# A decoder block on one core: the memory's keys and values kept on chip, the first output weights split first, the tokens' low parts made by VectorE, and the first gather written by token tiles

## The chip, the core and the metric

The kernel runs on one core of one Trainium2 chip. A core has four compute engines that each work through their own list in order: TensorE (PE in the profile, with PEld for its weight loads), VectorE (DVE), ScalarE (ACT) and GpSimd (POOL). SyncE (SP) only issues transfers, and GpSimd issues some as well; each engine's transfers start in the order of its list. The metric is the time of one execution in microseconds on the device; lower is better.

## The reference, cut to what matters

One decoder layer on 512 tokens of width 1024, in float32. The mixing stage projects the normed tokens, runs two branches (an RWKV-7 recurrence and a sparse attention), lifts and gates both and projects their sum. Then come cross-attention to 256 memory tokens and a mixture of 32 experts, of which each token uses 2.

```python
def hybrid_layer(h, mem, ...):
    z = rmsnorm(h, norm_mix) @ w_in
    z_rw, z_dsa, z_gate = _split(z, (RW_COLS, DSA_COLS, GATE_COLS))
    y_a = rwkv7_branch(z_rw, ...)
    y_b = dsa_branch(z_dsa, kv_norm, w_uk, w_uv)
    g_a, g_b = jnp.split(jax.nn.sigmoid(z_gate + b_gate), 2, axis=-1)
    h = h + (g_a * (y_a @ w_proj_a) + g_b * (y_b @ w_proj_b)) @ w_out
    h = h + cross_attention(rmsnorm(h, norm_cross), rmsnorm(mem, norm_mem), w_cq, w_ckv, w_co)
    h = h + hier_moe(rmsnorm(h, norm_ffn), ...)
    return h

def cross_attention(hn, mem_n, w_cq, w_ckv, w_co):
    q = (hn @ w_cq).reshape(B, S, X_HEADS, X_HEAD_DIM)
    k, v = jnp.split((mem_n @ w_ckv).reshape(B, M, 2, X_HEADS, X_HEAD_DIM), 2, axis=2)
    ...
    s = jnp.einsum('bshd,bmhd->bhsm', q, k).astype(jnp.float32) * (X_HEAD_DIM ** -0.5)
    p = jax.nn.softmax(s, axis=-1).astype(v.dtype)
    o = jnp.einsum('bhsm,bmhd->bshd', p, v).reshape(B, S, X_WIDTH)
    return o @ w_co

def hier_moe(hn, w_rg, b_rg, w_re, b_re, w_gate, w_up, w_down):
    g_prob = jax.nn.softmax((xt @ w_rg + b_rg).astype(jnp.float32), axis=-1)
    p_grp, grp = lax.top_k(g_prob, 1)
    ...
    p_e, e_loc = lax.top_k(jax.nn.softmax(e_logits, axis=-1), TOP_K_INNER)
    gate = p_grp * p_e / jnp.sum(p_e, -1, keepdims=True)
    ...
        hid = jax.nn.silu(xb @ w_gate[e]) * (xb @ w_up[e])
        return (hid @ w_down[e]) * gts[:, None].astype(xb.dtype)
```

## The kernel before, in words

All of it is one program for one core. Operands of a matmul are split into a high part (a rounded copy, `float32r`) and a low part (the rest), and a product is three matmuls: high by high, high by low, low by high. `split` makes both parts: ScalarE casts the high one, VectorE (or GpSimd, where the call says G) subtracts for the low one. Tokens are four tiles of 128 (`NT` = 4), features eight blocks of 128 (`KD` = 8).

The stages, with their place in the span of the profile: norms and transposes (0 to 40 us), the input projection with the recurrence and the indexer (40 to 390), the sparse attention `attend` (390 to 485), with the projection of the memory's keys as filler between its matmuls, the projection of the memory's values (485 to 513), the two lifts `w_pa` and `w_pb` (520 to 566), `w_out` (566 to 614), the queries, weights and values of the cross-attention (614 to 691), `w_co` with the routing (691 to 751), the first gather (751 to 765), the experts (766 to 1230) and the last norm.

Order. The program is written in the order of the stages, and a list scheduler then orders each engine's instructions; inside `tc.manual_schedule(engines={PE.engine})` TensorE keeps the written order. `behind(x)` makes what follows wait in the scheduler's list for instruction x. `M` is a free-list allocator over one big tile: `get` takes a place (with `top=True` from the upper end) and `done` gives it back; an instruction that writes to a place used before waits for that place's last readers and writers. `psum` takes the eight banks of PSUM in turn, by groups.

Memory's keys and values. `keys_values` loads 256 KB pieces of `w_ck` and `w_cv` through `ringm` (four raw buffers, two pairs of parts), which SyncE issues. ScalarE copies each result out of PSUM into a staging tile, and GpSimd's queue stores it to `kT_d` and `vm_d` in DRAM. After the lifts SyncE loads both back into `kT` and `vm`, and four splits of `kT` (cast by ScalarE, subtraction by GpSimd) make `kP`, the keys in two parts.

The lifts. For each of `w_pa` and `w_pb` the four blocks of the branch's output (`yaT`, `ybT`) are split into `act`, then four weights of 512 KB come through `ring2` (four raw buffers, three pairs of parts), each used for two groups of twelve matmuls. GpSimd's queue loads the gates from `gate_d`, and VectorE multiplies by them out of PSUM.

The routing. `tokmajor(w_co, ...)` writes a token tile at a time; after each, `after_cross` computes the logits (TensorE transposes L1079, logits L1083), adds them up (L1139, L1140), and `route` (L1089 to L1098) picks the group and the two experts on VectorE in steps of 4 to 32 columns. `parts` writes the token tile in two parts: ScalarE the high part (L1122) and a second full copy (L1123), GpSimd the difference (L1124). `place` (matmuls L1104, L1105) counts the tokens of earlier tiles for each expert, so that a token gets its row in the expert's block; tile t's placement needs tile t's choice.

The first gather. `choose(0)` makes a matrix of zeros and ones for the first four experts (L1166, one instruction for each token tile), and `gather(0, k)` multiplies the tokens by it: for each feature block k, a bank, eight matmuls over four token tiles and two parts, then a scaling by VectorE or ScalarE into `xgs`. All 64 matmuls carry line L1421. Then `turned` transposes the split gates (L1210) and the experts begin (L1452).

## Time and profile before

| | us |
|---|---|
| median of the timed runs (3) | 1271.01 |
| lowest and highest | 1266.04, 1273.87 |
| the profiled execution | 1261.12 |
| its span, first to last instruction | 1259.3 |
| TensorE busy | 1186.5 |
| VectorE, ScalarE, GpSimd busy | 647.8, 366.6, 111.1 |
| mean granted clock of TensorE | 0.965 of full speed |

The profiled execution is one run, 0.8% below the median of the timed ones; times inside the program are read from it. TensorE is busy 94% of the span, so an engine's work matters where TensorE waits for it. A granted clock of 1.00 is 2.4 GHz, one of 0.50 is 1.2 GHz.

### The profile page before, as it was taken

What the parts mean: (1) busy time and instruction counts of PE and PEld (TensorE: products, weight loads), DVE (VectorE), ACT (ScalarE), POOL (GpSimd) and SP (SyncE); (2) the same over time, 40 slices, a digit from 0 to 9 for tenths busy, and PEclk for the clock granted to TensorE, in tenths of its full rate; (3) what the DMA queues carried; (4) which work ended last, traced back from release to release, by engine and by line L of the source; (5) the groups of instructions that cost most, each with busy time, mean ns of one, the idle gap of its engine ahead of it and who ended that gap; (6) DMA issues with size and microseconds to landing.
All of it is one profiled execution on the core that took longest, in us unless ns stands there. A gap on an engine that the chain in (4) does not pass through costs nothing. (4 is left out here: it accounts for less than half of the span.)

```text
span 1259.3 us, 18869 instructions
## 1 busy us (share of the span) xinstructions
PE 1186.5 (94%) x7630; PEld 860.6 (68%) x7630; DVE 647.8 (51%) x1417; ACT 366.6 (29%) x666; POOL 111.1 (9%) x102
## 2 busy tenths in 40 slices
PE   5999998899998999799999979899999999999995
PEld 5877676677777877688786867566565656565662
DVE  5346689686686563565545373433233333333325
ACT  4442322434333543422444351101010101110113
POOL 1121211111122101200000030000000000000001
PEclk8999898999998999899999989999999999999998
DMA  4211113215533115473324316899999999999991
GB/s 163 91 60 34 54 56 109 79 53 185 193 113 109 55 34 196 155 245 98 131 75 145 128 68 268 337 413 419 419 421 420 420 421 421 419 421 420 362 364 67
DMA packets 52137, 272.06 MB, mean 216 GB/s; under 512 B 6064, under 2 KB 6208, under 8 KB 27728
## 3 DMA queue, kind: packets, MB, share of 16 engines
q1 hardware_dynamic: 48544, 259.21, 53.5%
q0 software_dynamic: 3504, 11.62, 2.6%
q8 instruction: 61, 1.00, 0.3%
q14 instruction: 28, 0.23, 0.1%
HBM read 261.37 MB, written 9.44 MB: 215 GB/s over the span
## 5 line engine op out<-in xcount | busy, mean ns | idle before, releaser
L230 PE MATMUL banks<-xparts 128*128 128x512 f32 x864 | 227.0, 413 | 2.2 <-DVE xparts L197 2.2
L230 PEld LDWEIGHTS banks<-xparts 128*128 128x128 f32 x864 | 164.5, 196 | 43.2 <-issue 3.7
L1452 PE MATMUL banks<-big 128*64 128x256 f32 x1616 | 180.3, 380 | 0.0
L1452 PEld LDWEIGHTS banks<-big 128*64 128x64 f32 x1616 | 115.8, 137 | 63.5 <-issue 8.0
L230 PE MATMUL banks<-weights,rounded 128*128 128x512 f32 x384 | 95.0, 401 | 0.0
L1480 PE MATMUL banks<-big 128*64 128x512 f32 x384 | 86.6, 595 | 1.4 <-issue 1.4
L230 PEld LDWEIGHTS banks<-weights,rounded 128*128 128x128 f32 x384 | 72.0, 191 | 15.2 <-issue 1.0
L1364 DVE TENSOR_TENSOR big<-big,banks 128x512 f32<-128x512 f32 x128 | 79.6, 681 | 4.7 <-PE banks L1362 4.7
L1457 ACT ACTIVATE slot<-banks 128x256 f32<-128x256 f32 x32 | 12.3, 385 | 225.0 <-PE banks L1469 121.1
L197 ACT CAST xparts<-rawring 128x1024 fp32r<-128x1024 f32 x38 | 39.8, 1046 | 121.0 <-PE banks L230 61.3
L1421 PE MATMUL banks<-chosen,rounded 128*128 128x256 f32 x512 | 66.0, 290 | 0.5 <-DVE big L1139 0.3
L197 DVE TENSOR_TENSOR weights<-big,weights 128x1024 fp32r<-128x1024 f32 x32 | 39.0, 1222 | 53.6 <-ACT weights L197 51.2
L1362 PE MATMUL banks<-chosen 128*128 128x512 f32 x256 | 66.5, 403 | 0.0
L1356 DVE SCALAR_TENSOR_TENSOR chosen<-banks,big,chosen 128x512 fp32r<-128x512 f32 x32 | 24.0, 750 | 82.2 <-ACT chosen L1355 82.2
L1421 PEld LDWEIGHTS banks<-chosen,rounded 128*128 128x128 f32 x512 | 64.5, 198 | 2.2 <-DVE big L1438 1.2
L1480 PEld LDWEIGHTS banks<-big 128*64 128x64 f32 x384 | 26.9, 137 | 53.1 <-issue 48.4
L197 POOL TENSOR_TENSOR xparts<-rawring,xparts 128x1024 fp32r<-128x1024 f32 x20 | 48.9, 2446 | 150.4 <-ACT xparts L197 142.7
L1355 ACT ACTIVATE chosen<-banks,big 128x512 fp32r<-128x512 f32 x32 | 22.0, 688 | 131.3 <-PE banks L1480 121.0
L1470 DVE COPY big<-banks 128x512 f32<-128x512 f32 x16 | 11.1, 692 | 89.5 <-PE banks L1469 89.5
L197 ACT CAST weights<-big 128x1024 fp32r<-128x1024 f32 x32 | 33.4, 1051 | 79.6 <-PE banks L230 33.4
L1362 PEld LDWEIGHTS banks<-chosen 128*128 128x128 f32 x256 | 47.7, 192 | 11.9 <-issue 1.6
L1437 DVE TENSOR_SCALAR chosen<-banks,big 128x512 fp32r<-128x512 f32 x16 | 12.0, 751 | 81.9 <-PE banks L1435 81.9
(406 smaller groups left out, 1808.7 us busy)
## 6 DMA issues: line engine op xcount, KB each, us to landing
big<-in_w_e_gate SPq DMA_DIRECT2D x51, 1024.0 KB, 13.5
big<-in_w_e_up SPq DMA_DIRECT2D x50, 1024.0 KB, 13.6
big<-in_w_e_down SPq DMA_DIRECT2D x48, 1024.0 KB, 12.4
rawring<-in_w_in SPq DMA_DIRECT2D x38, 512.0 KB, 3.5
slots<-in_w_e_up SPq DMA_DIRECT2D x14, 1024.0 KB, 15.2
slots<-in_w_e_gate SPq DMA_DIRECT2D x13, 1024.0 KB, 13.4
slots<-in_w_e_down SPq DMA_DIRECT2D x12, 1024.0 KB, 11.7
big<-in_x SPq DMA_DIRECT2D x8, 512.0 KB, 6.4
```

The source lines that it names most:

```text
L197: return S.copy(hi, src).ins, (eng or V).tensor_tensor(lo, src, hi.bitcast(F32), op=OP.subtract).ins
L230: r = PE.matmul(pt, st(a), mv(b), start=(first and i == 0), stop=(last and i == 2))
L1355: r = S.activation(YE[:, 0, nh, :], pd, AF.Copy, scale=g[:, :])
L1356: V.scalar_tensor_tensor(YE[:, 1, nh, :], pd, g[:, :], YE[:, 0, nh, :].bitcast(F32), op0=OP.mult, op1=OP.subtract)
L1362: PE.matmul(pc_[:, :], PT[:, t * P:(t + 1) * P], YE[:, x, nh, :], start=(x == 0), stop=(x == 1))
L1364: V.tensor_add(hh, hh, pc_[:, :])
L1421: PE.matmul(pt[:, 0:256], HL(x, t)[:, k // 4, k % 4, :], Pr_[:, t].rearrange("p e s -> p (e s)"), start=(t == 0 and x == 0), stop=(t == NT ...
L1437: V.tensor_scalar(PT[:, :], pa[:, :], slot_id[:, :], None, op0=OP.is_equal)
L1452: PE.matmul(pu[x][hf * 64:hf * 64 + 64, :], xgs[h4][:, k % 4, es_], w[:, k % 4, hf * 256:hf * 256 + 256], start=(k == 0), stop=(k == KD - 1))
L1457: S.activation(hd_[:, :], pu[0], AF.Silu)
L1470: V.tensor_copy(ht[:], ph[:, :].rearrange("p (j a s) -> p j a s", j=2, s=64))
L1480: PE.matmul(pd[j * 64:j * 64 + 64, :], ht[:, j, fb * 2 + hf, :], w[hf][j][:, fb, nh * 512:nh * 512 + 512], start=(kb == 0), stop=(kb == 3))
```

## The change

It has four parts.

1. `kT` and `vm` get their places in `M` before the attention, once the recurrence's tiles are given back, and ScalarE copies the results out of PSUM straight into them. The DRAM tiles, the twelve stores and the two loads are gone.
2. The first weight of `w_pa` is loaded and split ahead of the four blocks of `yaT`; the three products of each lift come in the order high by high, low weight by high tokens, high weight by low tokens. The splits of `kT` are put behind the last matmul of the first group of `w_pa`.
3. In `parts` the low part is one VectorE instruction (scale, then subtract the high part); ScalarE's second copy and GpSimd's subtraction are gone.
4. The first gather keeps four PSUM banks for all eight feature blocks and goes by token tiles: choice of tile t, then its 16 matmuls, with the placement of the last tile ahead of the last 16. `first_gather` then does the eight scalings.

```diff
+    for x in (St[0], St[1], Sp, *Xs, AR, ZV, ST, AA, zxg, g2, msk, pc):
+        x.done()
+    kT, vm = M.get(KD, NMEM, top=True), M.get(2, D, top=True)
...
-            S.copy(kst[nb % 2][:, :], pt[:, 0:NMEM])
-            nc.gpsimd.dma_start(kT_d[:, nb, :], kst[nb % 2][:, :])
+            S.copy(kT[:, nb, :], pt[:, 0:NMEM])
...
-                S.copy(vst[t][:, :], pts[t][:, :])
-                nc.gpsimd.dma_start(vm_d[:, t, half * 512:half * 512 + 512], vst[t][:, :])
+                S.copy(vm[:, t, half * 512:half * 512 + 512], pts[t][:, :])
...
+        w0 = ring2.load(wsrc[0]) if x == 0 else None
         for k in range(4):
             split(act[:, x, 0, k, :], act[:, x, 1, k, :], src[:, k, :])
         for j in range(4):
-            w = ring2.load(wsrc[j])
+            w = w0 if x == j == 0 else ring2.load(wsrc[j])
...
-                for a, b in ((0, 0), (0, 1), (1, 0)):
+                for a, b in ((0, 0), (1, 0), (0, 1)):
...
+                if x == nb == 0:
+                    first_pa = r.ins
...
-    kT, vm = M.get(KD, NMEM, top=True), M.get(2, D, top=True)
-    nc.sync.dma_start(kT[:, :, :], kT_d[:, :, :])
-    nc.sync.dma_start(vm[:, :, :], vm_d[:, :, :])
-    for k in range(0, KD, 2):
-        split(kP[:, 0, k:k + 2, :], kP[:, 1, k:k + 2, :], kT[:, k:k + 2, :], G)
+    with behind(first_pa):
+        for k in range(0, KD, 2):
+            split(kP[:, 0, k:k + 2, :], kP[:, 1, k:k + 2, :], kT[:, k:k + 2, :], G)
...
-            S.activation(hn[:, g], src, AF.Copy, scale=rs[:, t:t + 1])
-            G.tensor_tensor(lo, hn[:, g], hi.bitcast(F32), op=OP.subtract)
+            V.scalar_tensor_tensor(lo, src, rs[:, t:t + 1], hi.bitcast(F32), op0=OP.mult, op1=OP.subtract)
...
-    place(NT - 1)
...
-    chosen = choose(0)
+    gathered = [PS[:, i, :] for i in (2, 3, 4, 5)]
+    first = {}
+    with tc.manual_schedule(engines={PE.engine}):
+        for t in range(NT):
+            if t == NT - 1:
+                place(t)
+            chosen = choose(0, [t])
+            for k in range(KD):
+                for x in range(2):
+                    i = k // 2
+                    with behind(*first.get(i, [])):
+                        r = PE.matmul(gathered[i][:, k % 2 * 256:k % 2 * 256 + 256], HL(x, t)[:, k // 4, k % 4, :],
+                                      Pr_[:, t].rearrange("p e s -> p (e s)"), start=i not in first, stop=True,
+                                      skip_group_check=i in first)
+                    first.setdefault(i, [r.ins])
...
+    def first_gather():
+        for k in range(KD):
+            to, gain = xgs[k // 4][:, k % 4, :], C["norm_ffn"][:, k:k + 1]
+            src = gathered[k // 2][:, k % 2 * 256:k % 2 * 256 + 256]
+            if k % 2:
+                S.activation(to, src, AF.Copy, scale=gain)
+            else:
+                V.tensor_scalar(to, src, gain, None, op0=OP.mult)
...
-        for k in range(KD):
-            gather(0, k)
+        first_gather()
         turned()
```

Line numbers of the kernel after are up to some 20 off those of before (L228 there is L230 here, L1178 and L1435 together are L1421 and its scalings).

SyncE's queue from the loads of the attention's weights to those of `w_out`, before (`early` and `big` are tiles on chip, `in_` names are inputs):

```order
L223 DMA rawring<-in_w_in 128x1024
L797 DMA early<-in_w_uk 128x512
L798 DMA early<-in_w_uv 128x512
L223 DMA early<-in_w_ck 128x512 x16
L223 DMA early<-in_w_cv 128x512 x7
L901 DMA big<-kT_d 128x2048
L223 DMA early<-in_w_cv 128x512 x9
L223 DMA big<-in_w_pb 128x1024 x3
L902 DMA big<-vm_d 128x2048
L223 DMA big<-in_w_pb 128x1024
L1264 DMA big<-in_w_e_gate 128x2048
L223 DMA big<-in_w_out 128x1024 x6
```

And after:

```order
L221 DMA big<-in_w_pa 128x1024
L798 DMA early<-in_w_uk 128x512
L799 DMA early<-in_w_uv 128x512
L221 DMA early<-in_w_ck 128x512 x4
L221 DMA big<-in_w_pa 128x1024
L221 DMA early<-in_w_ck 128x512 x12
L221 DMA early<-in_w_cv 128x512 x16
L221 DMA big<-in_w_pb 128x1024 x4
L1275 DMA big<-in_w_e_up 128x2048 x2
```

The loads of `kT_d` and `vm_d` are gone, the sixteen loads of `w_cv` stand together, two of `w_pa`'s loads stand among those of the attention's weights and of the keys, and two expert loads stand ahead of `w_out`.

ScalarE's list from the copies of the values' first half (L837) to the lifts, before (`rounded` is `act`, `weights` the parts of a lift's weight, `cross` is `kP`):

```order
L837 COPY early<-banks 128x512 x2
L197 CAST memory<-early 128x512 x6
L837 COPY early<-banks 128x512 x2
L197 CAST cross<-big 128x512 x4
L197 CAST rounded<-big 128x512 x4
L197 CAST weights<-big 128x1024 x3
L197 CAST rounded<-big 128x512 x4
L197 CAST weights<-big 128x1024 x4
```

And after (L836 is the same copy):

```order
L836 COPY big<-banks 128x512 x2
L195 CAST memory<-early 128x512 x6
L195 CAST weights<-big 128x1024
L195 CAST rounded<-big 128x512 x2
L836 COPY big<-banks 128x512 x2
L195 CAST rounded<-big 128x512 x2
L195 CAST weights<-big 128x1024 x2
L195 CAST rounded<-big 128x512 x4
L195 CAST cross<-big 128x512
L195 CAST weights<-big 128x1024
L195 CAST cross<-big 128x512 x3
```

The first weight's cast and two of the tokens' casts stand ahead of the last value copies, and the casts of K behind two more weights.

TensorE's list at the end of the routing, before (L1104 and L1105 are a placement, L1079 and L1083 the last tile's logits, L1421 the gather, L1210 the transposes of `turned`, L1452 the experts):

```order
L1104 MATMUL banks<-big 128x32
L1105 MATMUL banks<-big 128x32
L1079 MATMUL banks<-big 128x128 x4
L1083 MATMUL banks<-big 128x36 x4
L1421 MATMUL banks<-chosen,rounded 128x256 x4
L1104 MATMUL banks<-big 128x32
L1105 MATMUL banks<-big 128x32
L1421 MATMUL banks<-chosen,rounded 128x256 x60
L1210 MATMUL banks<-big,slot 96x128 x4
L1452 MATMUL banks<-big 64x256 x64
```

And after (L1103 and L1104, L1078 and L1082, L1178, L1221 and L1472 in the same order):

```order
L228 MATMUL banks<-weights,rounded 128x512 x6
L1103 MATMUL banks<-big 128x32
L1078 MATMUL banks<-big 128x128 x4
L1178 MATMUL banks<-chosen,rounded 128x256 x4
L1082 MATMUL banks<-big 128x36 x4
L1178 MATMUL banks<-chosen,rounded 128x256 x3
L1104 MATMUL banks<-big 128x32
L1178 MATMUL banks<-chosen,rounded 128x256 x41
L1103 MATMUL banks<-big 128x32
L1104 MATMUL banks<-big 128x32
L1178 MATMUL banks<-chosen,rounded 128x256 x16
L1221 MATMUL banks<-big,slot 96x128 x4
```

Of the 64 gather matmuls 48 stand ahead of the last placement, where 4 stood, and 16 behind it.

## Rows read from the trace of the kernel before

**Rows 1.** The page, engine table: busy time, share of the span, instructions.

```profile
PE 1186.5 (94%) x7630; PEld 860.6 (68%) x7630; DVE 647.8 (51%) x1417; ACT 366.6 (29%) x666; POOL 111.1 (9%) x102
```

**Rows 2.** TensorE's waits: line, releaser: us in total, times, longest us.

```profile
PE banks L887 <- ACT weights L197: 7.5, 1, 7.5
...
PE banks L1105 <- DVE big L1098: 4.6, 2, 2.7
...
PE banks L517 <- DMA early<-in_w_uk: 3.9, 1, 3.9
...
PE banks L832 <- ACT memory L197: 2.7, 1, 2.7
```

**Rows 3.** Timeline of TensorE, 440 to 570 us: start, us, instruction, [idle before, releaser].

```profile
485.73 9.79 PE L832 MATMUL banks<-memory 128*128 128x512 f32 x42
498.21 2.93 PE L832 MATMUL banks<-memory 128*128 128x512 f32 x6 [2.70 <-ACT memory L197]
501.48 11.21 PE L832 MATMUL banks<-memory 128*128 128x512 f32 x48 [0.34 <-ACT early L837]
520.22 46.08 PE L887 MATMUL banks<-rounded,weights 128*128 128x512 f32 x192 [7.53 <-ACT weights L197]
```

**Rows 4.** Engine busy times (instructions) in stretches, TensorE's granted clock, DMA share, GB/s.

```profile
498.20:501.20 3.00, 2.93 (x6) 1.83 (x6) 1.37 (x2) 1.49 (x3) 0.00 (x0) 0.51 0.59 165
...
520.00:525.10 5.10, 4.88 (x12) 3.83 (x13) 5.10 (x7) 4.14 (x7) 0.00 (x0) 0.50 0.22 71
525.10:566.00 40.90, 40.90 (x182) 33.84 (x181) 27.47 (x38) 10.22 (x12) 3.24 (x6) 1.00 0.74 253
```

**Rows 5.** Timeline of SyncE's DMA queue, 470 to 545 us.

```profile
479.52 9.34 SPq L223 DMA_DIRECT2D early<-in_w_cv  x7
491.78 0.33 SPq L901 DMA_DIRECT2D big<-kT_d  x1
492.19 13.62 SPq L223 DMA_DIRECT2D early<-in_w_cv  x9
...
535.52 5.77 SPq L223 DMA_DIRECT2D big<-in_w_out  x2
```

**Rows 6.** DMA issues: count, KB each, median us from issue to landing.

```profile
early<-in_w_cv SPq DMA_DIRECT2D x16, 256.0 KB, 3.6
```

**Rows 7.** Timeline of all engines, 512 to 525 us.

```profile
512.50 1.07 ACT L837 COPY early<-banks 128x512 f32<-128x512 f32 x2 [2.33 <-PE banks L832]
...
514.47 4.92 POOL L197 TENSOR_TENSOR cross<-big,cross 128x512 fp32r<-128x512 f32 x4
...
517.69 4.07 DVE L197 TENSOR_TENSOR rounded<-big,rounded 128x512 fp32r<-128x512 f32 x4 [6.79 <-ACT rounded L197]
...
521.68 3.48 DVE L197 TENSOR_TENSOR weights<-big,weights 128x1024 fp32r<-128x1024 f32 x3
```

**Rows 8.** Timeline of all engines, 744.2 to 752.2 us.

```profile
744.29 2.52 POOL L1124 TENSOR_TENSOR rounded<-big,rounded 128x512 fp32r<-128x512 f32 x2 [3.89 <-ACT big L1123]
744.42 1.20 DVE L1092 TENSOR_SCALAR big<-big 128x4 f32<-128x4 f32 x1
...
747.85 0.41 PE L1105 MATMUL banks<-big 128*128 128x32 f32 x2 [1.89 <-DVE big L1098]
...
751.87 0.23 DVE L1092 TENSOR_SCALAR big<-big 128x4 f32<-128x4 f32 x1
```

**Rows 9.** Timeline of all engines, 754.5 to 766.5 us.

```profile
756.29 0.29 DVE L1181 TENSOR_TENSOR big<-big 128x128 f32<-128x128 f32 x1
...
756.52 8.98 PE L1421 MATMUL banks<-chosen,rounded 128*128 128x256 f32 x58 [0.25 <-DVE chosen L1166]
...
760.74 0.48 DVE L1427 TENSOR_SCALAR big<-banks,big 128x256 f32<-128x256 f32 x1 [1.66 <-PE banks L1421]
...
762.53 0.28 DVE L1200 TENSOR_TENSOR slot<-big,chosen 128x128 f32<-128x128 f32 x1
...
765.87 0.87 PE L1452 MATMUL banks<-big 128*64 128x256 f32 x6
```

More of the change, by code (lines that the diff above doesn't have):

```diff
@@ L102, in build @@
     q_d = park.tile([P, 4, T], F32, name="q_d")
-    kT_d = park.tile([P, KD, NMEM], F32, name="kT_d")
-    vm_d = park.tile([P, 2, D], F32, name="vm_d")
     M = Mem(pool.tile([P, NBIG], F32, name="big"), NBIG)
@@ L802, in build @@
     ringm = Ring([MX.get(512) for _ in range(4)], [KR.get(2, 512) for _ in range(2)])
-    kst, vst = [MX.get(NMEM) for _ in range(2)], [MX.get(512) for _ in range(2)]
     def keys_values():
@@ L852, in build @@
         pass
-    for x in (St[0], St[1], Sp, *Xs, AR, ZV, ST, AA, zxg, g2, msk, pc, cw, cT, cb, *isc_.values()):
+    for x in (cw, cT, cb, *isc_.values()):
         x.done()
@@ L883, in build @@
                 pt = psum()
-                for a, b in ((0, 0), (0, 1), (1, 0)):
+                for a, b in ((0, 0), (1, 0), (0, 1)):
                     for k in range(4):
                         o = (n * 4 + k) * P
-                        PE.matmul(pt[:, :], w[:, a, o:o + P], act[:, x, b, k, :], start=(a + b + k == 0), stop=(a == 1 and k == 3))
+                        r = PE.matmul(pt[:, :], w[:, a, o:o + P], act[:, x, b, k, :], start=(a + b + k == 0),
+                                      stop=(b == 1 and k == 3))
+                if x == nb == 0:
+                    first_pa = r.ins
                 if x == 0:
@@ L1046, in build @@
     hT = [[growt[:, i * T:i * T + T] for i in range(x, 4, 2)] for x in range(2)]
-    hn = M.get(2, 4, P)
     ring = hg2 + [M.get(2048, top=True) for _ in range(6)] + [XC.get(2048) for _ in range(3)]
@@ L1160, in b3, with choose @@
         return ap.unsqueeze(2).to_broadcast([P, ap.shape[1], n])
-    def choose(b):
-        for t in range(NT):
-            with behind(*routed if b == 0 and t == NT - 2 else []):
-                r = V.tensor_tensor(Pr_[:, t], i64[:, :].unsqueeze(1).to_broadcast([P, 4, 64]),
-                                    pos[:, t, b * 4:b * 4 + 4].unsqueeze(2).to_broadcast([P, 4, 64]), op=OP.is_equal)
-        return r.ins
-    chosen = choose(0)
-    for x in (junk, wr, ss, rs, rneg, upper, rows, small, ohg, off, wg, left, seen, top2, ss0, Lp, hn):
+    def choose(b, ts_=range(NT)):
+        for t in ts_:
+            r = V.tensor_tensor(Pr_[:, t], i64[:, :].unsqueeze(1).to_broadcast([P, 4, 64]),
+                                pos[:, t, b * 4:b * 4 + 4].unsqueeze(2).to_broadcast([P, 4, 64]), op=OP.is_equal)
+        return r.ins
+    gathered = [PS[:, i, :] for i in (2, 3, 4, 5)]
+    first = {}
+    with tc.manual_schedule(engines={PE.engine}):
+        for t in range(NT):
+            if t == NT - 1:
[9 more added lines that the diff above has]
+                    first.setdefault(i, [r.ins])
+    for x in (junk, wr, ss, rs, rneg, upper, rows, small, ohg, off, wg, left, seen, top2, ss0, Lp):
         x.done()
```

## The prediction

> **What bounds the kernel now.** I read the page's engine table first: TensorE is busy 1186.5 of 1259.3 us [rows 1], so time can only come out of the 73 us in which it is idle, or out of stretches in which it runs at its lower clock. The list of TensorE's waits says which idle pieces the change can reach [rows 2]: 7.5 us at the first matmul of w_pa, 4.6 us in two waits of the routing, 3.9 us for w_uk, 2.7 us inside the projection of the memory's values. Then the timeline of TensorE around the first and the last of these [rows 3] and the granted clock of the same stretches [rows 4]: the reader is to see that a gap costs more than its length. After the 2.70 us gap at 498.21 six matmuls take 2.93 us at a clock of 0.51, where 48 take 11.21 us (0.234 each) in the steady stretch; after the 7.53 us gap at 520.22 the clock is 0.50 for 5.1 us, and 12 matmuls take 4.9 us in place of 2.8. Behind the 0.34 us gap at 501.48 nothing is lost. So the stages up to the routing are bound by TensorE with two holes, the routing by VectorE's chain of small steps, and the experts by TensorE again.
>
> The profiled execution took 1261.12 us, 1.8 us above its span; the median of the timed runs, 1271.01, lies 0.8% above it. I sum on the profiled execution and carry the difference over to the median.
>
> **1. Keys and values stay on chip.** The twelve stores and two 1 MB loads go. What counts is where one of the loads stood: SyncE issued seven w_cv loads (479.52 to 488.86, one per 1.33 us), then the load of kT_d at 491.78, which has to wait for kT_d's last store, and only then the eighth w_cv load at 492.19 [rows 5]. TensorE ran out of values at 495.5 [rows 3]. Without that load the eighth is due 1.33 us behind the seventh, near 490.2, lands 3.6 us later [rows 6], at 493.8, and needs one cast of about 0.6 us: ready before 495.5. The ring of four buffers then goes round in 3.6 plus a cast and a subtraction, about 4.9 us, against 4 x 1.40 = 5.6 us that TensorE takes for four loads (96 matmuls of 0.234 are 22.4 us for 16), so it should stay ahead. To be had: 2.7 of gap and 2.93 - 6 x 0.234 = 1.5 of low clock, 4.2 in all. I take **3.5**, because the ring has little slack; bounds 0 and 4.5. The stores cost TensorE nothing now and so give nothing. SyncE's queue also loses the load of vm_d; two expert loads of 1 MB now stand ahead of w_out's loads, which were issued at 535.52 [rows 5] and are first used when w_pb ends, at 520.22 + 46.08 = 566.3 [rows 3]: 30 us of cover, cost nothing.
>
> In the order the third w_pa load, 512 KB, now stands ahead of w_uk's, for which TensorE already waits 3.9 us [rows 2]. At the pace of the w_cv loads (256 KB per 1.33 us) it can put w_uk back by 2.7 us at most, and by nothing where the w_uk load has other things to wait for. No row decides; I take **1.0 lost**, bounds 0 and 2.7.
>
> **2. First weight of w_pa split first.** In before, ScalarE's last value copies (512.50, two in 1.07) are followed by four casts of K, four of tokens and the weight's, for which the first matmul waits [rows 2], and VectorE's low parts come behind these (517.69, 521.68) [rows 7]. After, ScalarE casts w0 (about 1.1 us, as two of the 512-wide copies of 0.54) and two token blocks before the last value copies, in the 2.33 us in which it was idle. The copies then stand half a us later, 513.05 to 514.1. TensorE's first w_pa matmul waits for the first copy, since that frees its bank: 513.6, a gap of 0.9 us in place of 7.5. The products with the weight's low part come second and the tokens' low parts last: casts three and four end near 515.2, VectorE's four subtractions of 0.58 to 0.69 (three of 1024 columns take 3.48 [rows 7]) near 516, the twelfth matmul near 517.3. In before it ended at 525.1 [rows 4]. That is 7.8 us; I take **7.5**. Bounds: 9.6 if the gap (7.5) and the low clock (2.1) both vanish, 5 if the clock falls in the short gap and the casts come a little later.
>
> The four splits of K move under w_pa. ScalarE's part is small. GpSimd's four take 4.92 us, and in before VectorE's four subtractions beside them took 4.07 us in place of some 2.8 [rows 7], so about one GpSimd instruction of waiting got into them. Under w_pa and w_pb VectorE is busy 27.5 of 40.9 us [rows 4], which leaves 13.4; TensorE did not wait there once. On GpSimd's queue three of these splits (3.7 us) stand ahead of gate loads, and behind a late gate stands the VectorE step that frees a bank. I charge 0, bounds 0 and 2.5.
>
> The Trainium skill (SBUF — State Buffer, section "SBUF: two separate sides") says that a VectorE instruction with two SBUF inputs and a GpSimd instruction that reads SBUF take one shared port pair in turn, and that the loser waits for the whole instruction. The 4.07 us fit it. By the rule alone the four splits could hold VectorE up by their whole 4.92 us in their new place, and the sum below would shrink by that; by the rows they fall into idle time.
>
> **3. Low parts by VectorE.** ScalarE loses eight copies that nobody waits for. GpSimd loses its eight subtractions of 1.26 us each. While these run, VectorE's tiny steps of the routing stand still: L1092 takes 1.20 us at 744.42 and 0.23 us at 751.87, when GpSimd has not begun [rows 8]. Two such stalls per token tile, about 1 us each, go; two VectorE instructions of 512 columns, about 0.6 to 0.7 each, come into the same chain. Only the last two tiles lie on the path (w_co's matmuls cover the others). Gain 2 x (2 x 1.0 - 2 x 0.65) = 1.4 at best, and as much lost where a stall had been hidden. I take **0**, bounds -1.5 and +1.5.
>
> **4. First gather by token tiles.** In before 58 of the 64 gather matmuls run from 756.52 on in 8.98 us, behind two waits of the placement (2.7 us the longer [rows 2]), and the experts begin at 765.87 [rows 9]. After, 48 of 64 are written ahead of the last tile's placement and fill its wait. That placement ends no earlier than before, near 755.5: at the 0.155 us each of the 58, the 41 matmuls between it and the placement before, which ran at 747.85 [rows 8], take 6.4 us, as long as VectorE's chain. The last choice is then made at about 756.5 and the last 16 matmuls end by 759, in place of 765.5. But the gate transposes and the experts stand behind another chain, which the gather used to cover: from 756.29 to 762.81 VectorE made the exponentials' sums and split the gates, and only 1.66 us of that was waiting for gather results [rows 9]. So about 5 us after the last choice, at 761.5, the transposes can start, and the experts at 762.0, 3.9 us earlier. TensorE has by then idled some 2.5 us, and the two gaps above cost 1.5 and 2.1 us of low clock behind them [rows 4]: 1.7 off. I take **2.2**, bounds -1 (the chain is longer by the new scalings of the gather, all eight of which now come at once) and 5 (no idle time).
>
> **Sum.** 3.5 - 1.0 + 7.5 + 0 + 2.2 = 12.2 us: 1261.12 becomes 1248.9, and the median 1271.0 becomes 1258.7 (12.3 off); I write 1258.5. The scheduler also writes the stages before 390 us in a slightly different order; the waits there are of the same kind as the 3.9 us one, and I allow 2 us either way. This measurement can tell about 1%, 12.7 us, from no change, so the sum lies on that line.
>
> **The rivals.**
> - *The values' gap was the ring's, not the load's.* For it: loads at 1.33 us each against a need of 1.40, next to no slack. Against it: SyncE's own order, with the gap exactly behind the kT_d load [rows 5]. Then 3.5 are missing: 1262.1.
> - *The K splits hold VectorE up under w_pa.* For: 4.07 us instead of 2.8 [rows 7]. Against: 13.4 us of idle VectorE. At the full 4.92 us: 1263.5. The rule of the SBUF page named above is this rival's mechanism.
> - *The gate chain takes the whole gain of the gather*, or the low clock behind the new gap does. For: the chain is serial on VectorE and ScalarE. Against: half of it was padded by gather waits. Then 2 to 3 are missing: 1261.
> - *More than the sum:* no idle time before the experts (5 in place of 2.2), the value gap wholly gone, w_uk untouched: 4.5 + 7.8 + 5 = 17.3, 1253.6.
> - *Slower: w_out behind the expert loads.* The second of the two 1 MB loads ahead of w_out takes the place of the sparse branch's output. If it were released only when w_pb ends (now near 555.3), both loads (eight times 1.33, 10.6 us) and w_out's own 2.7 would follow, and 2.1 for the split: TensorE gets its weight near 571, 15.4 us late, and loses 2.1 more by its clock. That ends 5 us slower, 1276. It decides once w_out's first load is issued after about 560. Against it: that output is last read by the token splits, some 40 us earlier.
> - *That it doesn't do what it says:* the order shows the w_cv loads in one piece and 48 gathers ahead of the placement, so this has no share of its own.
>
> **Chances.** The forecast 0.42 (it spreads over 1254 to 1263, half of it past the 1% line), the ring 0.10, the held VectorE 0.07, the gate chain 0.14, more 0.21, slower 0.06. Faster by over 1%: 0.23 + 0.21 = 0.44. Within 1%: 0.19 + 0.31 = 0.50. Slower: 0.06. The range runs from 1247, below the "more" case with 2 us for the early stages and the runs' own scatter, to 1268, above the rivals that miss one term.
>
> **What would show it.** Right: no gap over 0.5 us between the values' matmuls; the first w_pa matmul within 1.5 us of the last value matmul and a clock near 1.00 behind it; w_uk's wait 4 to 6 us; the experts' first matmul some 16 us earlier in the span less what w_uk costs; a TensorE wait of 2 to 4 us at the gate transposes. Wrong: a wait for DMA in the values, clock 0.5 in the first 5 us of w_pa, or a loss in the reordered stages before 390 us.

## The result, and the profile after

The change makes the kernel a little faster: 1258.97 us is the median of eleven runs (1254.86 to 1262.30) against 1266.65 of before (1260.88 to 1273.87), a ratio of 0.9931 with the 95% interval 0.9909 to 0.9953, or 8.7 us (6 to 11.5). The forecast was 12.3 us less than before, 1258.5.

The two profiled executions alone would have told another story. That of after takes 1261.4 us, span 1259.6, as long as the profiled execution of before. In the stages it looks like this.

The list of TensorE's waits of after answers to [rows 2]; columns as there. L886 is w_pa's matmul, L515 the attention's first, L1221 the gate transposes, L831 the values.

```profile
PE banks L515 <- DMA early<-in_w_uv: 5.8, 1, 5.8
...
PE banks L886 <- DVE big L892: 2.8, 1, 2.8
PE banks L1221 <- DVE slot L1211: 2.5, 1, 2.5
...
PE banks L886 <- ACT big L836: 0.9, 1, 0.9
...
PE banks L831 <- ACT big L836: 0.7, 1, 0.7
```

The 7.5 us ahead of w_pa have become 0.9, the 2.7 us in the values have become 0.7, and the two waits on the placement too. New are 2.8 us inside w_pa, behind L892 (VectorE's step that frees a bank), and 2.5 us ahead of the gate transposes; the wait for the attention's weights has grown from 3.9 to 5.8 us.

TensorE's timeline of after, 440 to 620 us, answers to [rows 3].

```profile
497.38 11.15 PE L831 MATMUL banks<-memory 128*128 128x512 f32 x48
509.27 11.17 PE L831 MATMUL banks<-memory 128*128 128x512 f32 x48 [0.74 <-ACT big L836]
521.31 11.39 PE L886 MATMUL banks<-rounded,weights 128*128 128x512 f32 x48 [0.87 <-ACT big L836]
535.45 34.49 PE L886 MATMUL banks<-rounded,weights 128*128 128x512 f32 x144 [2.75 <-DVE big L892]
569.77 32.81 PE L228 MATMUL banks<-weights,rounded 128*128 128x512 f32 x144
```

The values take 23.1 us from 497.38 to 520.44, where before took 27.0, and w_pa begins 0.87 us later. Then the reader is to see two things: the gap of 2.75 us in the middle of w_pa, and that the values begin 11.7 us later than in before (485.73). So in this pair the front of the kernel lost what its middle gained.

The clock of w_pa in windows of after answers to [rows 4]: 1.00 at the start, and low only behind the new gap.

```profile
520.00:533.00 13.00, 11.83 (x50) 8.71 (x49) 12.72 (x12) 10.14 (x18) 5.57 (x5) 1.00 0.52 163
...
535.40:541.00 5.60, 5.55 (x18) 4.48 (x19) 2.92 (x4) 0.00 (x0) 0.57 (x1) 0.70 0.99 394
```

SyncE's queue answers to [rows 5]: sixteen value loads in one piece, and a load of w_pa ahead of that of w_uk.

```profile
400.67 0.33 SPq L221 DMA_DIRECT2D big<-in_w_pa  x1
401.90 0.33 SPq L798 DMA_DIRECT2D early<-in_w_uk  x1
...
491.00 22.56 SPq L221 DMA_DIRECT2D early<-in_w_cv  x16
```

TensorE's timeline at the end of the routing answers to [rows 9].

```profile
750.93 5.16 PE L1178 MATMUL banks<-chosen,rounded 128*128 128x256 f32 x41
...
757.29 2.14 PE L1178 MATMUL banks<-chosen,rounded 128*128 128x256 f32 x16 [0.84 <-DVE chosen L1162]
761.94 1.09 PE L1221 MATMUL banks<-big,slot 128*96 128x128 f32 x4 [2.51 <-DVE slot L1211]
762.95 15.14 PE L1472 MATMUL banks<-big 128*64 128x256 f32 x128
```

The experts begin at 762.95, 2.9 us earlier than in before, though the values began 11.7 us later. From w_out's first matmul (569.77, in before 566.13) to the experts it is 193.2 us against 199.7.

### The profile page after: what moved, and what is told of

Read it like the earlier page. It is cut to its first block, busy times and chain, and to the rows that moved or that the text cites. A ratio compares the mean times of both kernels' runs of the same rounds, so it can differ in the third digit from the quotient of the medians.

```text
span 1259.6 us, 18805 instructions
## 1 busy us (share of the span) xinstructions
PE 1188.2 (94%) x7630; PEld 859.0 (68%) x7630; DVE 649.7 (52%) x1425; ACT 362.4 (29%) x658; POOL 93.9 (7%) x82
## 5 line engine op out<-in xcount | busy, mean ns | idle before, releaser
L228 PE MATMUL banks<-xparts 128*128 128x512 f32 x864 | 231.1, 417 | 4.5 <-DVE xparts L195 4.5
L228 PEld LDWEIGHTS banks<-xparts 128*128 128x128 f32 x864 | 165.2, 197 | 46.3 <-DVE xparts L195 5.3
L1472 PE MATMUL banks<-big 128*64 128x256 f32 x1616 | 181.4, 381 | 0.0
L1472 PEld LDWEIGHTS banks<-big 128*64 128x64 f32 x1616 | 116.2, 138 | 64.5 <-issue 9.2
L228 PE MATMUL banks<-weights,rounded 128*128 128x512 f32 x384 | 93.2, 396 | 0.0
L228 PEld LDWEIGHTS banks<-weights,rounded 128*128 128x128 f32 x384 | 70.8, 188 | 14.7 <-issue 1.0
L1477 ACT ACTIVATE slot<-banks 128x256 f32<-128x256 f32 x32 | 12.3, 384 | 226.1 <-PE banks L1489 121.1
L195 DVE TENSOR_TENSOR weights<-big,weights 128x1024 fp32r<-128x1024 f32 x32 | 42.7, 1338 | 56.0 <-ACT weights L195 53.5
L1441 PEld LDWEIGHTS banks<-chosen,rounded 128*128 128x128 f32 x448 | 54.5, 192 | 1.4 <-DVE big L1458 1.2
L1441 PE MATMUL banks<-chosen,rounded 128*128 128x256 f32 x448 | 55.2, 284 | 0.0
## 6 DMA issues: line engine op xcount, KB each, us to landing
big<-in_w_e_down SPq DMA_DIRECT2D x48, 1024.0 KB, 12.3
slots<-in_w_e_down SPq DMA_DIRECT2D x12, 1024.0 KB, 12.3
```

The source lines that it names most:

```text
L195: return S.copy(hi, src).ins, (eng or V).tensor_tensor(lo, src, hi.bitcast(F32), op=OP.subtract).ins
L228: r = PE.matmul(pt, st(a), mv(b), start=(first and i == 0), stop=(last and i == 2))
L1441: PE.matmul(pt[:, 0:256], HL(x, t)[:, k // 4, k % 4, :], Pr_[:, t].rearrange("p e s -> p (e s)"), start=(t == 0 and x == 0), stop=(t == NT ...
L1472: PE.matmul(pu[x][hf * 64:hf * 64 + 64, :], xgs[h4][:, k % 4, es_], w[:, k % 4, hf * 256:hf * 256 + 256], start=(k == 0), stop=(k == KD - 1))
```

## The experiments

Each kernel was timed against before on the same chip, in five rounds. The table gives the ratio to before, and from each profiled execution (one each) the start of the attention (first matmul with w_uk) and the lengths of the stages that follow, cut at the first matmul of the values, of w_pa, of w_out and of the experts, and at the end of the span.

| kernel | ratio (95%) | attention starts | to values | to w_pa | to w_out | to experts | to end |
|---|---|---|---|---|---|---|---|
| before | 1 | 393.4 | 92.3 | 34.5 | 45.9 | 199.7 | 493.4 |
| after | 0.9931 (0.9909, 0.9953) | 406.6 | 90.8 | 23.9 | 48.5 | 193.2 | 496.7 |
| x_places | 1.0050 (1.0028, 1.0072) | 402.6 | 90.5 | 33.3 | 46.3 | 199.8 | 492.8 |
| x_keys_alone | 0.9961 (0.9941, 0.9981) | 401.7 | 90.7 | 25.5 | 46.2 | 198.6 | 495.2 |
| x_stores | 0.9952 (0.9930, 0.9975) | 405.4 | 90.6 | 25.5 | 46.8 | 199.9 | 496.1 |
| x_no_keys | 0.9950 (0.9926, 0.9973) | 396.5 | 92.2 | 31.2 | 46.8 | 193.2 | 493.8 |
| x_low_parts | 0.9960 (0.9937, 0.9983) | 404.4 | 91.7 | 34.2 | 46.4 | 196.3 | 493.0 |
| x_gather | 0.9981 (0.9957, 1.0005) | 398.4 | 92.1 | 34.3 | 45.7 | 197.9 | 495.9 |
| x_free_late | 0.9927 (0.9901, 0.9953) | 399.2 | 90.3 | 23.9 | 48.5 | 194.7 | 497.8 |
| x_ksplit | 0.9880 (0.9847, 0.9912) | 404.4 | 91.1 | 23.9 | 43.9 | 194.3 | 497.7 |
| x_turn | 0.9880 (0.9852, 0.9908) | 401.8 | 90.8 | 23.9 | 48.5 | 189.6 | 496.1 |
| x_late_turn | 0.9883 (0.9854, 0.9912) | 401.7 | 90.4 | 23.9 | 43.8 | 192.6 | 495.4 |
| x_three | 0.9845 (0.9815, 0.9874) | 397.1 | 90.9 | 23.9 | 43.9 | 193.0 | 495.5 |
| x_load_order | 0.9845 (0.9811, 0.9878) | 404.2 | 92.3 | 23.9 | 43.9 | 192.7 | 495.9 |

The stages from the attention to w_out repeat from kernel to kernel within 0.8 us where the kernels agree there, the stage up to the experts within 1.5 us. The start of the attention does not, and that has to be known to read it: before, x_no_keys, x_gather, x_low_parts and x_load_order have the same TensorE list up to the end of the values, and begin the attention at 393.4, 396.5, 398.4, 404.4 and 404.2.

**Where the first 11 us went.** The first part of the change gives the recurrence's tiles back earlier. The allocator then lays the normed memory, which had a place of its own, on a tile of the recurrence, so its steps wait for that, and the scheduler writes the stages from 230 us on in another order.

```diff
+    for x in (St[0], St[1], Sp, *Xs, AR, ZV, ST, AA, zxg, g2, msk, pc):
+        x.done()
+    kT, vm = M.get(KD, NMEM, top=True), M.get(2, D, top=True)
...
-    kT, vm = M.get(KD, NMEM, top=True), M.get(2, D, top=True)
     nc.sync.dma_start(kT[:, :, :], kT_d[:, :, :])
```

> The kernel before, with one thing of the change: the recurrence's tiles are given back ahead of the attention's inputs and kT and vm get their places there and then; everything is still parked in DRAM and loaded back. By the allocator the normed memory then lies on a tile of the recurrence, where it had a place of its own. Theory of the place: this alone reorders the stages from 230 us to the attention and costs what the profile of after shows there, so the attention's first matmul (393.4 us in before, 406.6 in after) comes at 402 to 407 us, and the time is 8 to 13 us above before (ratio 1.006 to 1.010). Rival, chance of the clock: the 11 us are one execution's granted clock; ratio 0.998 to 1.002.

It is 6.3 us slower (3.5 to 9.1), below the 8 to 13 that the first theory named, and clearly not the rival's 0. The other way round, the same three lines moved behind the norm of the memory in after:

```diff
-    kT, vm = M.get(KD, NMEM, top=True), M.get(2, D, top=True)
...
     nm = mem_norm()
+    for x in (St[0], St[1], Sp, *Xs, AR, ZV, ST, AA, zxg, g2, msk, pc):
+        x.done()
+    kT, vm = M.get(KD, NMEM, top=True), M.get(2, D, top=True)
```

> After, with three lines moved: the recurrence's tiles are given back and kT and vm placed only once the memory is normed, so the normed memory has its old place, all four loads of w_pa stand ahead of w_uk by far, and the stages up to the attention are ordered as before. Theory of the place: the attention's first matmul comes at 392 to 396 us, the values run without a gap, and the time is 8 to 13 us below after, 16 to 22 us below before (ratio 0.983 to 0.988). Chance of the clock: as after, 0.991 to 0.995.

The attention starts at 399.2, not at 392 to 396, and the ratio is that of after within its interval, although the lists of all four compute engines are those of before again up to there. So the 11 us of the profiled pair are only in part the order's. TensorE's list is the same in all fourteen kernels up to 238 to 243 us. From its end there to the attention, the seven kernels with before's order (before, x_no_keys, x_gather, x_low_parts, x_free_late, x_three, x_load_order) take 154.3 to 161.4 us, 157.6 in the mean; the seven with after's (after, x_places, x_keys_alone, x_stores, x_ksplit, x_turn, x_late_turn) take 160.7 to 166.2, 163.0 in the mean. That is 5.4 us for the order, of which 1.0 is a longer wait for the attention's weights and most of the rest low clock (one minus the granted clock, times the length of the stretch, is 10.2 us in the mean, in place of 6.5). The timed runs don't agree on it: the order costs 6.3 us in x_places, some 5 between x_late_turn and x_three, and 0.5 between x_free_late and after, so its size stays open. The profiled execution of before starts the attention earliest of all fourteen, and stood 5.5 us under the later median of its own kernel.

**The keys' part alone, and the change without it.**

```diff
-            S.copy(kst[nb % 2][:, :], pt[:, 0:NMEM])
-            nc.gpsimd.dma_start(kT_d[:, nb, :], kst[nb % 2][:, :])
+            S.copy(kT[:, nb, :], pt[:, 0:NMEM])
```

> The kernel before with the first part alone: keys and values stay on chip. Theory of the place: the values' gap goes (3.9 us gained), the stages ahead of the attention lose some 11 and the wait for the attention's weights grows by 2: 5 to 10 us above before (ratio 1.004 to 1.008). Chance of the clock: 3 to 5 us below before (0.996 to 0.998).

> After without its first part: keys and values are parked and loaded back as before, the other three parts are in. Theory of the place: the stages up to the attention run as before (first matmul of the attention at 393 to 395 us), the gap in the values' projection stays (3 to 4 us), w_pa and the routing gain 4 to 9 and 5 to 7 us: 9 to 15 us below before, faster than after by 2 to 7 us (ratio to before 0.988 to 0.993). Chance of the clock: slower than after by the 3.9 us that the values' gap costs, ratio 0.995 to 0.998.

Both are faster than before, the one by 4.9 us (2.4 to 7.5), the other by 6.3 (3.4 to 9.4). The theory of the place had the first slower and the second faster than it is; both ratios lie at the edge of the range named for the chance of the clock, but not for its reason. The table shows that: with the keys on chip, and no other part, the stretch from the values to w_pa is 9.0 us shorter, not 3.9. The rest is in front of w_pa: its wait is 2.4 us there and still 6.0 us in x_no_keys, where the first weight is split first. All engines of x_no_keys at that place:

```profile
513.69 1.07 ACT L837 COPY early<-banks 128x512 f32<-128x512 f32 x2 [2.33 <-PE banks L832]
514.57 1.07 POOL L838 DMA_DIRECT2D vm_d<-early  x2 [10.56 <-ACT early L837]
514.65 2.18 ACT L197 CAST cross<-big 128x512 fp32r<-128x512 f32 x4
...
518.22 1.04 ACT L197 CAST weights<-big 128x1024 fp32r<-128x1024 f32 x1 [1.39 <-DMA vm_d<-early]
...
519.84 6.54 PE L888 MATMUL banks<-rounded,weights 128*128 128x512 f32 x14 [5.96 <-ACT rounded L197]
```

ScalarE has the weight's cast ready to go behind four casts of K and waits another 1.39 us for the store of vm_d. The parts of the lifts lie in the space of the pool `early`, closed just before (`early.close()` in the kernel), and the staging tiles, which the store still reads, lay in that pool. In before the tokens' casts stand behind the same wait:

```profile
517.04 2.17 ACT L197 CAST rounded<-big 128x512 fp32r<-128x512 f32 x4 [1.40 <-issue]
```

In the five kernels that still have the staging tiles (before, x_places, x_no_keys, x_low_parts, x_gather) the first cast for the lifts begins 0.14 to 0.15 us after the last store of vm_d has landed (in before at 516.90), some 3.5 us after the last value copy; the four casts of K only fill 2.2 us of that. In x_keys_alone the tokens' casts wait for nothing of the kind and stand ahead of the last value copies:

```profile
513.74 2.18 ACT L195 CAST rounded<-big 128x512 fp32r<-128x512 f32 x4 [0.76 <-DVE memory L195]
...
515.83 1.06 ACT L836 COPY big<-banks 128x512 f32<-128x512 f32 x2
516.79 2.94 ACT L195 CAST weights<-big 128x1024 fp32r<-128x1024 f32 x3
```

So the 3.5 us up to the store's landing and the 2.2 us of the tokens' casts, less half a us by which the copies come later, make up the 5.1 us by which the gap is shorter there. x_stores puts the twelve stores back, from kT and vm themselves:

```diff
             S.copy(kT[:, nb, :], pt[:, 0:NMEM])
+            nc.gpsimd.dma_start(kT_d[:, nb, :], kT[:, nb, :])
```

> x_keys_alone (before with the first part alone) with the twelve stores to DRAM put back, read by nobody: they read kT and vm where these now lie, not the staging tiles. TensorE's, VectorE's and ScalarE's lists are those of x_keys_alone. Theory of the place: in before the casts for w_pa waited because their tiles overlap the staging tiles, which the stores still read; with stores from another place the wait ahead of w_pa stays 2 to 3 us as in x_keys_alone, and the time too (ratio to before 0.994 to 0.998). Rival: the stores' own traffic and GpSimd's time made the wait; then it is 6 to 8 us again, and the ratio 1.000 to 1.003.

The wait stays at 2.39 us (its row of TensorE's timeline below) and the ratio is that of x_keys_alone. It was the place that the stores read from, not the stores: here they land at 523.74, and no cast waits for them.

```profile
521.38 9.85 PE L889 MATMUL banks<-rounded,weights 128*128 128x512 f32 x36 [2.39 <-ACT weights L197]
```

**The K splits.** In after all engines at 529 us show VectorE's subtraction for a weight at 4.91 us in place of 1.2, beside three of GpSimd's K splits, and L892, which frees a bank, only behind it:

```profile
529.19 4.91 DVE L195 TENSOR_TENSOR weights<-big,weights 128x1024 fp32r<-128x1024 f32 x1
529.23 3.79 POOL L195 TENSOR_TENSOR cross<-big,cross 128x512 fp32r<-128x512 f32 x3
...
534.62 0.68 DVE L892 SCALAR_TENSOR_TENSOR big<-big,banks 128x512 f32<-128x512 f32 x1
```

```diff
-    with behind(first_pa):
+    with behind(last_gate, last_half):
         for k in range(0, KD, 2):
             split(kP[:, 0, k:k + 2, :], kP[:, 1, k:k + 2, :], kT[:, k:k + 2, :], G)
```

Here last_gate is GpSimd's last gate load and last_half ScalarE's last split of the mix. `behind` sets the order on the engine of the instruction that it names, so behind a TensorE matmul it had moved nothing on ScalarE and GpSimd.

> After, with the four splits of K queued behind the last gate load on GpSimd and the last split of the mix on ScalarE, so they run under w_out; TensorE's and VectorE's lists are those of after, instruction for instruction. Theory of the held VectorE: the 2.75 us wait in w_pa and the low clock behind it come from GpSimd's subtractions, beside which one of VectorE took 4.9 us; both go, w_pa and w_pb take 46 us, and the time is 3 to 5 us below after (ratio to before 0.989 to 0.991). Rival: the splits hold VectorE up as much under w_out, where TensorE then waits, or the gain is taken back in the experts: ratio as after, 0.992 to 0.995.

w_pa and w_pb run through in 44.0 us without a gap:

```profile
519.46 44.03 PE L887 MATMUL banks<-rounded,weights 128*128 128x512 f32 x192 [0.87 <-ACT big L837]
```

The ratio is 0.9880 against 0.9931, and from w_pa to w_out it is 4.6 us less than in after. The rival does not hold: under w_out TensorE waits no longer than before.

**The gate transposes.**

```diff
         first_gather()
-        turned()
...
             hidden = gate_up(p * 2)
+            if p == 0:
+                turned()
```

> After, with the gate transposes moved behind the first expert's gate and up products. Theory of the gate chain: the 2.5 us wait ahead of them and the low clock behind it go, the first expert's first matmul comes at 759 to 760.5 in the span of after in place of 762.95, and the time is 2 to 4 us below after (ratio to before 0.989 to 0.992). Rival: the branch at the end of the second pair of experts, where TensorE waited 5.6 us, or the stream of expert weights takes it back: ratio as after, 0.992 to 0.995, with that wait 2 us longer.

The first expert begins behind the gather without the 2.5 us wait, and by the table 3.6 us earlier in its stage than in after; the transposes cost 0.6 us later. (With the same edit the stage is only 0.2 to 0.6 us shorter in x_late_turn, x_three and x_load_order, where the clock was lower: see the last section.) The ratio is again 0.9880.

```profile
754.64 7.13 PE L1472 MATMUL banks<-big 128*64 128x256 f32 x64
761.70 0.64 PE L1221 MATMUL banks<-big,slot 128*96 128x128 f32 x4
```

**The two parts of the routing.**

```diff
-            S.activation(hn[:, g], src, AF.Copy, scale=rs[:, t:t + 1])
-            G.tensor_tensor(lo, hn[:, g], hi.bitcast(F32), op=OP.subtract)
+            V.scalar_tensor_tensor(lo, src, rs[:, t:t + 1], hi.bitcast(F32), op0=OP.mult, op1=OP.subtract)
```

> The kernel before with the third part alone, the tokens' low parts by VectorE. The prediction's step: VectorE's stalls beside GpSimd and its new instructions cancel, 0 within 1.5 us (ratio 0.999 to 1.001). Rival: part of the 6.6 us that after gains from w_out's start to the first expert comes from here, since the stalls of 1 us stood in the chain of every tile's routing and let the clock fall: 2 to 4 us below before (0.997 to 0.998).

> The kernel before with the fourth part alone, the first gather by token tiles. The prediction's step: 2 us below before, bounds -1 and 5 (ratio 0.996 to 1.001), with a wait of 2 to 4 us at the gate transposes. Rival: most of the 6.6 us gained from w_out's start to the first expert comes from here: 5 to 7 us below before (0.9945 to 0.996).

The low parts alone gain 5.1 us (2.2 to 8), 3.4 of them between w_out and the experts; the gather alone 2.4 (-0.6 to 5.4), 1.8 of them there. Together (x_no_keys, after) the stage is 6.5 us shorter, 1.3 more than the sum. A single execution does not tell these so finely: the four kernels with before's instructions there (before, x_places, x_keys_alone, x_stores) take 198.6 to 199.9 us, the four with after's (after, x_no_keys, x_free_late, x_ksplit) 193.2 to 194.7. So neither the gather's 1.8 nor the 1.3 is clear of chance. TensorE's idle time in the stage says more: 8.1 us in before and in x_gather, 6.1 in x_low_parts, 6.3 in after. TensorE's timeline of before has a wait of 1.21 us for the second tile's logits and then 15 matmuls of w_co in 5.28 us:

```profile
734.65 0.64 PE L1083 MATMUL banks<-big 128*128 128x36 f32 x4 [1.21 <-DVE big L1080]
...
736.01 5.28 PE L230 MATMUL banks<-weights,rounded 128*128 128x512 f32 x15
```

With the low parts by VectorE there is no such wait, the same 15 take 3.70 us, and the last placement's wait is 2.28 us in place of 2.69. The wait is the change's; the low clock behind it is this execution's: x_places, x_keys_alone, x_stores and x_gather have the same wait of 1.19 to 1.21 us, and the clock stays at 1.00 over the 10.5 us behind it.

```profile
740.35 3.70 PE L230 MATMUL banks<-weights,rounded 128*128 128x512 f32 x15
...
761.75 0.64 PE L1104 MATMUL banks<-big 128*128 128x32 f32 x2 [2.28 <-DVE big L1097]
```

In x_gather the 43 matmuls ahead of the placement take 7.95 us, where 41 take 5.16 in after at full clock, and the wait for the gate chain is there as well:

```profile
753.92 7.95 PE L1180 MATMUL banks<-chosen,rounded 128*128 128x256 f32 x43
...
767.73 0.64 PE L1223 MATMUL banks<-big,slot 128*96 128x128 f32 x4 [2.52 <-DVE slot L1213]
```

**Put together.** x_late_turn has the edits of x_ksplit and x_turn, x_three that of x_free_late as well, x_load_order also this:

```diff
+        with behind(*[uv_load] if ri[0] <= 12 else []):
             nc.sync.dma_start(w, I[nm][e, hf])
```

> After, with both the K splits under w_out and the gate transposes behind the first expert. Theory: the two are in different stages and add, 5 to 9 us below after (ratio to before 0.982 to 0.988). Rival: the branch wait or the weights' stream gives one of them back: 0.987 to 0.991.

> As x_late_turn, and with the recurrence's tiles given back only once the memory is normed (the edit of x_free_late). Theory of the place, cut to what x_free_late showed: 2 to 5 us below x_late_turn (ratio to before 0.979 to 0.986). Rival, that the order of the early stages makes no difference beyond an execution's clock: as x_late_turn within 2 us.

> As x_three, and with the first expert loads queued behind the load of w_uv on SyncE, so that no big load stands ahead of the attention's first weights. Theory of the queue: the wait at the attention's first matmul (5.6 to 5.8 us in after, 3.9 in before) is back at 2.5 to 4 us, and the time is 1 to 3 us below x_three. Rival: the wait is set by the last gate store, behind which the w_uk load stands in any order: 5 to 6 us, no gain.

x_late_turn is no faster than either of its edits; x_three is the best, with x_load_order, 19.6 us below before (16 to 23.4) and about 11 below after. In x_load_order the wait for the attention's weights is 4.2 us in place of 5.8, close to what the theory of the queue says, but the 1 to 3 us below x_three did not come: the ratio is that of x_three. Its profiled execution is the slowest of its six and starts the attention at 404.2, with before's lists on the compute engines up to there.

## Why the prediction was right, and where it was not

The range, the direction and nearly the size came true, but the sum holds together because steps that were off cancel. That 1258.97 lies so close to 1258.5 is luck: before's median of three runs, 1271.01, from which the forecast was carried over, became 1266.65 with eleven, and the gain is 8.7 us, not 12.3. Of the signs named for being right, four came: the short wait ahead of w_pa, the full clock behind it, w_uk's wait and the wait at the gate transposes. Two did not: the gap in the values is 0.74 us, not under 0.5, and the experts begin 2.9 us earlier in the profiled pair, not some 16 less w_uk's loss. One sign of being wrong came, the loss before 390 us.

- **Values (3.5 us forecast).** 3.9 us against before, 2.1 to 3.7 against the four other kernels that keep the load: the gap was the kT_d load's, the ring keeps up. Right; the rival of the ring is out.
- **First weight of w_pa (7.5 us, bounds 5 and 9.6).** The size is right, 6.7 us of gap and 2.0 of low clock, since w_pa and w_pb take 43.9 us once the K splits are away. The reason was wrong. The step that failed is "The stores cost TensorE nothing now and so give nothing": the casts for w_pa waited for vm_d's stores to be done with the staging tiles. The first part alone brings 5.1 us of the gap, the second alone 1.6, so the order of casts that the forecast put down to the second part came mostly by the first.
- **K splits under w_pa (0, bounds 0 and 2.5).** They cost 4.6 us, outside the bounds: 2.75 of wait and the rest low clock. "which leaves 13.4" us of idle VectorE was the failing step. An average over 41 us says nothing of the first 15, in which VectorE must make the low parts of three weights and seven token blocks and free four banks. Three GpSimd subtractions took 3.79 us, and the VectorE one beside them took 3.7 us longer than its 1.2: it ended 1.1 us after the last of the three. The rule of the Trainium skill (SBUF — State Buffer, section "SBUF: two separate sides"), that the loser waits for the whole instruction, agrees, but here VectorE waited through three instructions in a row. This rival had 0.07.
- **w_uk (1.0 lost, bounds 0 and 2.7).** 1.9 lost in the profiled pair; x_load_order gets 1.6 of it back. In all fourteen kernels the load is issued 0.44 us after the last gate store has landed; what differs is its own landing, 2.6 to 3.8 us later in the five kernels with no large load just ahead of it (before, x_no_keys, x_low_parts, x_gather, x_load_order), 4.0 to 4.7 in the nine with one. Against the loss stands what the forecast had no term for: the attention itself takes 90.7 us in the mean in the nine kernels with another TensorE list there than before's, and 92.1 in the five with before's, 1.4 us less. Most of that is TensorE's idle time (0.3 to 0.9 us in the nine, 1.6 to 2.3 in the five); why is not shown.
- **Low parts (0, bounds -1.5 and 1.5).** 3.4 us gained in the stage, 2.0 of them idle time of TensorE and the rest clock. "Only the last two tiles lie on the path" failed: the stalls beside GpSimd made TensorE wait for the second tile's logits as well, and in before's profiled execution the clock fell behind that wait.
- **Gather by tiles (2.2, bounds -1 and 5).** 1.8 alone and 3.1 with the low parts, by single executions; alone, the timed runs cannot tell it from 0. The wait for the gate chain came as forecast, 2.51 us, and took what was saved of the placement's wait: TensorE's idle time in the stage is that of before.
- **Early stages ("I allow 2 us either way").** By the means above this is about as large a miss as the K splits: 4.4 us beyond the wait for the weights; x_places has 6.3 us with the wait, but x_free_late gets only 0.5 back. x_free_late shows that the place of the three lines makes the order: with them behind the memory's norm, before's order up to the attention is there again. That it works through the normed memory's place is read from the allocator, not shown.
- **Experts.** No term, but 2.8 us more to the branch behind the second pair: 1.1 at the low clock behind the gate chain's wait and 1.7 in the wait at the branch, 5.6 us in place of 3.9. That wait is 3.4 to 3.9 us in four kernels and 5.3 to 5.8 in ten, and goes with no single part (x_gather 5.4, x_no_keys, which has the same gather, 3.6). The DMA packets in the traces show what ends it: in all fourteen a 16 KB load on the queue that the page calls instruction, and the wait ends 3.0 to 3.1 us behind this load. The load begins 0.5 to 0.7 us ahead of the wait in the four and 1.3 to 1.7 us into it in the ten; what sets that stays open.

With the means of the early stages (5.4, the wait for the weights in it) and of the attention (1.4) the terms that the runs show give 3.9 + 8.7 - 4.6 - 5.4 + 1.4 + 6.5 - 2.8 = 7.7, in the interval of 6 to 11.5. That is a check of the size and no proof of each term: the routing's 6.5 is 5.7 by the means of four kernels each.

## What to carry to other kernels

A store keeps its source tile busy until it lands: what it costs is seen at whoever next writes to that place, so a staging tile in a pool whose space the next stage takes over is a wait in that stage. Freeing a tile earlier can move another one onto it and reorder stages far ahead of the edit; compare the order of the whole program, not of the edited stage. When work is put beside a busy stage, hold it against the busiest few us of that stage and against the engine it shares a path with, not against the stage's mean.

## What the runs showed that was not expected

The same instructions do not always meet the same clock. TensorE's clock can be low with no idle time at all: in after it is 0.79 from 318 to 342 us while the profile shows TensorE busy throughout, in a stretch where 66 of the 102 matmuls and transposes have 64 columns. What lowers it there was not tried.

```profile
318.00:326.00 8.00, 8.00 (x38) 4.75 (x37) 4.73 (x13) 1.31 (x3) 0.29 (x1) 0.79 0.25 90
326.00:334.00 8.00, 8.00 (x37) 4.97 (x36) 2.50 (x7) 0.78 (x1) 0.00 (x0) 0.79 0.01 2
334.00:342.00 8.00, 8.00 (x32) 5.83 (x32) 4.25 (x9) 5.07 (x7) 0.56 (x1) 0.79 0.66 207
```

And the same wait has a different sequel. In eight of these kernels (after, x_no_keys, x_free_late, x_ksplit, x_turn, x_late_turn, x_three, x_load_order) TensorE's list at the end of the routing is the same, with the same wait of 1.74 to 1.76 us for the last tile's logits. In x_turn the clock stays at 1.00 over the 10.5 us behind it:

```profile
743.75:754.25 10.50, 9.66 (x80) 9.50 (x81) 8.15 (x42) 4.21 (x8) 0.00 (x0) 1.00 0.33 110
```

In x_three it is 0.67:

```profile
734.75:745.25 10.50, 10.50 (x62) 10.42 (x63) 6.07 (x31) 3.88 (x7) 0.00 (x0) 0.67 0.29 101
```

It held in three of the eight (after, x_no_keys, x_turn), where the 41 gather matmuls took 5.16 us, and fell in five, where they took 6.2 to 7.0; at 0.67 some 3.5 of the 10.5 us are lost. What decides it was not tried. The clock is a good part of why single executions of one kernel differ by 7 to 13 us: among the eleven of after the shortest (1254.86 us) had a mean clock of 0.968, the longest (1262.30) 0.961, a difference that is worth 8.8 us over 1255, where the two differ by 7.4. And gains of two edits that each remove a wait need not add in one execution, as x_late_turn shows, whose clock fell there where x_turn's held; whether that is the whole reason, the intervals are too wide to say.
